# A feed-forward block with one product fewer by recursion: a product moved back, a fixed order on the matrix engine, and four row tiles prepared later

## The chip, the core and the metric

The kernel runs on one core of a Trainium2 chip. The core has a matrix engine (TensorE, "PE" in the profile, with its weight loads as "PEld"), a vector engine (VectorE, "DVE"), a scalar engine (ScalarE, "ACT"), a general engine (GpSimd, "POOL") and a queue that issues transfers (SyncE, "SP"). Each has its own list of instructions and works through it in order; semaphores tie the lists together. PE writes to a small memory of its own with banks (PSUM), which DVE and ACT read. The metric is the time of one execution on the device in microseconds (us); lower is better.

## What is computed

One layer of a transformer-like block over 2048 rows of 1024 numbers. Two kinds of attention come first; their heads' outputs are joined, multiplied by an output matrix and added to the input. Then comes the part that this document is about:

```
u2   = rms_norm(h, norm2_w)             # 2048 x 1024
gate = u2 @ w_gate                       # 1024 x 2816
up   = u2 @ w_up                         # 1024 x 2816
h    = h + (silu(gate) * up) @ w_down    # 2816 x 1024
```

The answer is asked for in 32-bit floating point. The kernel gets near that on 16-bit matrix products by splitting every operand into a high and a low half (hi + lo) and adding three products: hi*hi, hi*lo and lo*hi.

## The kernel before, in words

The attention part and the output projection fill the time up to about 1427 us. What follows is the feed-forward. The 2816 hidden columns are taken in 11 groups of 256, and the 2048 rows in two halves of 1024, so there are 22 steps: groups 0 to 10 for the first half, then the same for the second (the list `steps`, the loop variable `i`).

**Seven products for eight.** In each step, gate and up are each a product of 1024 x 1024 by 1024 x 256, cut into 2 x 2 blocks. A scheme after Strassen and Winograd forms it with seven block products, at the price of sums of the blocks before and after. `quad` issues the seven for gate or for up: `pa`, `p6`, `p7`, `pd`, then one more added into the bank of `pa`, `p4`, and a seventh added into the bank of `pd`. Each block product is twelve matmuls (four slices of the depth, three pairs of halves), all issued by `product`. Between them DVE adds and subtracts: L1047 after the second product, L1052 after the third, L1057 after the fourth (it reads `pd`, and the seventh product may only add into that bank after this), L1067 after the sixth, L1071 after the seventh. Silu of the gate is on ACT (L1083), the product of gate and up on DVE (L1103), and the result is split into an `act` tile (two buffers) by ACT casts and subtractions on POOL or DVE (L98).

**Down.** Each time two groups have their `act` (after the gate of the next step), `down` multiplies both by their `w_down` blocks, again with seven block products, for four row groups j of 256 rows; a block product is three matmuls for each group ("unit"), so six here. The down at the change of the halves has one unit, the last has three. Its products are named `pa`, `pb`, `pc`, `pd`, one more into `pa`, one more into `pd`, and `pe`. DVE adds the banks onto tiles `hs` with rows of h (L1144), which SP loads from memory and stores back (L1128, L1187); there are four such tiles, two for each j.

**Weights.** In the first half, every group's three weight blocks are fetched, scaled, summed and split (`load_ffn`: squares on ACT L954 or L190 into the one `sq` tile, column sums `fsc` on PE L963, splits on ACT L216 and DVE L221, sums on POOL L98), a group ahead of their use, and stored; in the second half they are fetched back ready. Gate and up weights share two buffers (tag wgu), down weights have two (tag wd). The steps of this work hang on hooks: `quad` calls `at(1)` to `at(7)` after its products, and `in_gate` and `in_up` then advance the chains of the next weights.

**Late rows.** The normalized, transposed and block-summed rows (X) come from memory; for the last four row tiles (12 to 15) they are made during the feed-forward by the generator `build_x`, in two passes of two tiles. Each `tick` advances it by one `yield`: load, norm, transposes on PE (L1213), then casts, subtractions and stores to the memory tensor `xcd`. It uses the four `hs` tiles and, as a 16-bit buffer, one of the two wd buffers. `late_at` names the hooks of the first two steps at which it ticks. X of the second half is loaded at the twelfth step (`load_x`, L1225) into the same tiles as that of the first half, in the order `XL = (0, 4, 5, 1, 2, 6, 3)`; each tile is free when the last product of the first half that reads it is done.

**Order.** The program is written in a framework that turns it into the lists of the engines by simulating it: an instruction goes out when the simulation has it ready, the one written first ahead of others. So the products need not run in the order in which they are written. `tc.issue_after(x)` adds an edge: instructions within it come later than x on the same engine, without a wait. Before, only the column sums and transposes stand in such edges (`behind()`, which refers to `front[0]`, the last matmul issued), and the products themselves are free.

Of the kernel before, what the change touches and what calls it, by code (L numbers as in the profile page):

```python
# [40 lines left out]
CU = 3  # L41
# [18 lines left out]
def block(tc, a, out):  # L60
# [3 lines left out]
    with top:  # L64
# [809 lines left out]
        with ExitStack() as ph2:  # L874
# [21 lines left out]
            rows = []  # L896
# [8 lines left out]
            def stage(fg, nme):  # L905
                st = stages[:, turn[0]]
                turn[0] ^= 1
                f0 = 256 * fg
                with tc.issue_after(rows[1].ins) if (fg, nme) == (1, "u") else nullcontext():
                    fetch(st, f0, nme)  # L910
                store(0)
                return st
# [113 lines left out]
            def product(ps_, wv, wo, X, xo, start, stop):  # L1026
                q = 0
                for kt in range(4):
                    for xi, wi in ((0, 0), (1, 0), (0, 1)):
                        front[0] = PE.matmul(ps_[:].rearrange("p (t n) -> p t n", n=P), lhsT=wv[:, wo, wi, 128 * kt : 128 * kt + 128], rhs=X[xo][:, :, xi, kt, :], start=start and q == 0, stop=stop and q == 11, skip_group_check=not start).ins  # L1030
                        q += 1

            def quad(wv, X, tag, bufs, c11, hooks):
# [13 lines left out]
                DVE.tensor_tensor(u2[:], p6[:], u2[:], ALU.add)  # L1047
                at(2)
# [21 lines left out]
                product(pd, wv, 5, X, 3, False, True)  # L1070
                DVE.tensor_tensor(u2[:], u2[:], pd[:], ALU.add)  # L1071
                c11(0, 1, u2)
                at(7)

            def gate(W, X, hooks):
# [10 lines left out]
                quad(W["g"], X, "cg", 5, on_gate, hooks)  # L1086
                note("A", 2000)
                return sg

            def up(W, X, sg, hooks, final=False):  # L1090
                if final:
                    act = stages[:].rearrange("p b n -> p (b n)").bitcast(F16)[:, :7168].rearrange("p (o s n) -> p o s n", o=7, s=2)
                else:
                    act = fp.tile([P, 7, 2, 512], F16, tag="act", bufs=2, name=nm("act"))
# [23 lines left out]
                quad(W["u"], X, "cu", CU, on_up, hooks)  # L1118
# [12 lines left out]
            def down(half, units, hs, last, hook=None):  # L1131
# [3 lines left out]
                def prod(po, ao, wo, j, start=True):  # L1135
                    for u, (W, act) in enumerate(units):
                        for q, (xi, wi) in enumerate(((0, 0), (0, 1), (1, 0))):
                            front[0] = PE.matmul(po[:], lhsT=act[:, ao, xi, 128 * j : 128 * j + 128], rhs=W["d"][:, wo, wi, :], start=start and u == 0 and q == 0, stop=u == nu - 1 and q == 2, skip_group_check=not start).ins  # L1138
# [13 lines left out]
                for j in range(4):  # L1152
# [14 lines left out]
                    acc(u2[:], pb, u2[:])  # L1167
                    pc = pst("pd")
# [177 lines left out]
```

## Time and profile before

| | us |
|---|---|
| median of three runs | 2686.87 |
| lowest, highest | 2677.16, 2687.23 |
| the profiled execution | 2682.59 |
| its span, first to last instruction | 2680.8 |
| PE busy in the span | 2492.4 (93%) |
| DVE busy | 1932.7 (72%) |
| POOL busy | 1489.1 (56%) |
| ACT busy | 1347.0 (50%) |
| granted PE clock, mean | 0.984 |

The profile is that of one execution. A matmul's row starts when it is issued, and matmuls overlap, so that the start of the next row tells more than the length of one. Idle time before an instruction is put down to what ended it. The chain of work that ended last lies on PE for 39% of the span in the rows that the page sums up, most of it in the products of lines 1030 (gate and up) and 1138 (down).

### The profile page before, as it was taken

The page shows a single profiled execution, that of the slowest core. Times are in us where ns is not written, and L with a number is a line of the kernel's source. Part 1 is how long each engine was busy: PE and PEld are TensorE (multiplying, and loading weights), DVE is VectorE, ACT ScalarE, POOL GpSimd, SP SyncE. Part 2 cuts the span into 40 slices and gives each one's busy share as a digit, 9 for nine tenths or more (in the row PEclk, how much of TensorE's full clock was granted, in tenths as well). Part 3 has the DMA queues.
Part 4 walks back from the last instruction along what each step waited for, and adds up shares of the span by engine and source line. Part 5 has one row for each costly group of instructions (what it writes and reads, how often), then busy time and mean ns, then how long its engine had stood idle before and what let it go on. Part 6 is the DMA issues. An engine that isn't in the chain of part 4 may idle for free. (4 is left out here: it accounts for less than half of the span.)

```text
span 2680.8 us, 50579 instructions
## 1 busy us (share of the span) xinstructions
PE 2492.4 (93%) x19628; PEld 1498.6 (56%) x19628; DVE 1932.7 (72%) x3711; ACT 1347.0 (50%) x2487; POOL 1489.1 (56%) x1098
## 2 busy tenths in 40 slices
PE   6998989888988989889989899999999999999999
PEld 4655656577776776557775344444444444444444
DVE  6898969898989989877766868777685544444434
ACT  4665656567978878665644535344352112111121
POOL 2578667667767766546764656565564232322323
PEclk9999999999999999999999899999999999999999
DMA  6777697767998979987897574665649743635532
GB/s 222 213 162 181 146 200 168 179 143 184 193 179 179 185 160 209 210 191 217 218 285 282 208 250 178 255 226 202 245 183 346 293 177 143 233 141 186 195 111 95
DMA packets 619585, 534.41 MB, mean 199 GB/s; under 512 B 480640, under 2 KB 548224, under 8 KB 609104
## 3 DMA queue, kind: packets, MB, share of 16 engines
q1 hardware_dynamic: 617520, 529.09, 69.9%
q8 instruction: 154, 2.52, 0.4%
q0 software_dynamic: 512, 1.36, 0.2%
q14 instruction: 87, 0.71, 0.1%
q10 hardware_dynamic: 1312, 0.72, 0.1%
HBM read 261.08 MB, written 147.32 MB: 152 GB/s over the span
## 5 line engine op out<-in xcount | busy, mean ns | idle before, releaser
L98 POOL TENSOR_TENSOR s<-z,s 128x1024 f16<-128x1024 f32 (+7 forms) x288 | 472.0, 1647 | 142.5 <-ACT s L89 109.8
L507 PE MATMUL sc<-kT,qT 128*128 128x512 f16 (+3 forms) x1520 | 382.0, 353 | 53.3 <-DVE z L623 19.3
L622 DVE TENSOR_TENSOR_SCAN z<-z,sc 128x512 f32<-128x512 f32 (+3 forms) x320 | 352.8, 1112 | 58.6 <-ACT sc L620 38.0
L1138 PE MATMUL pd<-wd,act 128*128 128x512 f16 x1764 | 390.9, 379 | 1.2 <-DVE cg L1071 1.2
L326 PE MATMUL pj<-w,xt 128*128 128x384 f16 x1920 | 352.2, 331 | 18.8 <-ACT xt L683 6.9
L1030 PEld LDWEIGHTS <-wg 128*128 128x128 f16 x1848 | 182.0, 99 | 230.2 <-issue 16.4
L518 PE MATMUL yp<-v,aT 128*128 128x64 f16 (+1 forms) x4896 | 269.8, 204 | 41.6 <-DMA aT<-s 40.2
L518 PEld LDWEIGHTS <-aT 128*128 128x128 f16 x4896 | 237.5, 99 | 120.4 <-DMA aT<-s 52.5
L1030 PEld LDWEIGHTS <-wu 128*128 128x128 f16 x1848 | 180.7, 98 | 218.0 <-issue 2.6
L98 POOL TENSOR_TENSOR act<-cg,act 128x512 f16<-128x512 f32 x112 | 148.5, 1337 | 262.9 <-ACT act L1097 150.8
L1138 PEld LDWEIGHTS <-act 128*128 128x128 f16 x1764 | 172.8, 98 | 209.4 <-issue 2.8
L326 PEld LDWEIGHTS <-xt 128*128 128x128 f16 x1920 | 187.3, 99 | 147.5 <-issue 21.4
L89 ACT CAST s<-z 128x128 f16<-128x128 f32 (+7 forms) x215 | 173.1, 809 | 134.1 <-DMA aT<-s 40.5
L98 POOL TENSOR_TENSOR hs<-hs,cu 128x512 f32<-128x512 f32 x99 | 130.9, 1328 | 171.3 <-DVE hs L1144 70.8
L619 ACT ACTIVATE z<-sc,c 128x512 f32<-128x512 f32 (+3 forms) x320 | 210.7, 663 | 25.6 <-PE sc L507 11.7
L1097 ACT CAST act<-cg 128x512 f16<-128x512 f32 x126 | 77.3, 616 | 238.4 <-DVE cg L1103 162.7
L507 PEld LDWEIGHTS <-qT 128*128 128x128 f16 x1520 | 128.4, 99 | 121.0 <-DVE z L623 23.0
L832 PE MATMUL po<-wo,mt 128*128 128x256 f16 x1536 | 180.7, 277 | 13.9 <-DVE xf L835 8.4
L1030 PE MATMUL pm<-X,wu 128*128 128x512 f16 x792 | 180.4, 379 | 1.3 <-DVE wu L221 1.3
L1030 PE MATMUL pm<-X,wg 128*128 128x512 f16 x792 | 181.3, 382 | 0.0
L342 PE MATMUL pj<-xt,w 128*128 128x128 f16 x2304 | 175.0, 220 | 6.7 <-DVE v L364 5.7
L1144 DVE SCALAR_TENSOR_TENSOR hs<-pd,c,hs 128x512 f32<-128x512 f32 x136 | 99.0, 747 | 109.6 <-PE pd L1138 83.1
(266 smaller groups left out, 4737.6 us busy)
## 6 DMA issues: line engine op xcount, KB each, us to landing
xt<-xs SPq DMA_DIRECT2D x112, 512.0 KB, 4.3
hs<-hd SPq DMA_DIRECT2D x68, 512.0 KB, 4.5
hd<-hs SPq DMA_DIRECT2D x56, 512.0 KB, 4.7
split<-wg SPq DMA_DIRECT2D x11, 1792.0 KB, 7.8
split<-wu SPq DMA_DIRECT2D x11, 1792.0 KB, 6.7
split<-wd SPq DMA_DIRECT2D x11, 1792.0 KB, 7.2
wg<-split SPq DMA_DIRECT2D x11, 1792.0 KB, 7.3
wd<-split SPq DMA_DIRECT2D x11, 1792.0 KB, 12.2
```

Of the source, the lines that this page charges most:

```text
L89: ACT.copy(dst, src)
L98: (DVE if e == "D" else POOL).tensor_tensor(dst, a_, b_, op)
L326: PE.matmul(pj[:, :384], lhsT=xv[:, xi, kt, :], rhs=G["w"][:, wi, kt, :], start=n == 0, stop=n == 23)
L342: PE.matmul(o, lhsT=x_ if c == 2 else w_, rhs=w_ if c == 2 else x_, start=n == 0, stop=n == 23)
L507: last = PE.matmul(sc[:, : 128 * w].rearrange("p (t n) -> p t n", n=P), lhsT=G["q"][i // 4][:, a_, i % 4, :], rhs=G["k"][q][:, b_, 0:w, :] ...
L518: PE.matmul(yp[:, y0 : y0 + wd], lhsT=aT[:, a_, :], rhs=v[:, v_ : v_ + wd], start=start and j == 0 and q == 0, stop=stop and j == nb - 1 a ...
L619: ACT.activation(om[:, lo:hi], sc[:, :w], AF.Sigmoid, scale=G["nkz"][:])
L622: DVE.tensor_tensor_scan(ov, ov, sc[:, :w], om[:, hi : hi + 1], op0=ALU.mult, op1=ALU.bypass)
L832: PE.matmul(po[:, sl], lhsT=mt[:, kt, P * xi : P * xi + P], rhs=wos[2 * h + n][wi][:, kt, :], start=q == 0, stop=q == 23)
L1030: front[0] = PE.matmul(ps_[:].rearrange("p (t n) -> p t n", n=P), lhsT=wv[:, wo, wi, 128 * kt : 128 * kt + 128], rhs=X[xo][:, :, xi, kt, : ...
L1138: front[0] = PE.matmul(po[:], lhsT=act[:, ao, xi, 128 * j : 128 * j + 128], rhs=W["d"][:, wo, wi, :], start=start and u == 0 and q == 0, s ...
L1144: DVE.scalar_tensor_tensor(dst, po[:], kd[:], src, op0=ALU.mult, op1=ALU.add)
```

## The change

Three edits go together.

1. `quad` hands the seventh product back as a function (`seventh`) when called with `late=True`, which `gate` does. It is run behind the second product of what follows: of `down` at j = 0 where a down is due, else of `up`. The hook `at(7)` of the gate comes before it.
2. `product` and down's `prod` issue all their matmuls within `behind()`. So every block product is issued on PE after the one written before it.
3. `build_x` ticks in steps 2 to 5 (the third to sixth group) and not in 0 and 1. Each pass takes its four `hs` tiles anew, fetches the gain anew, and uses the `act` tile of the step as its 16-bit buffer, which `up` then takes over (`acts`), in place of a wd buffer. The first tick before the loop is gone, and so is the edge that held the fetch of the second group's up weights behind the late rows' loads.

```diff
             def product(ps_, wv, wo, X, xo, start, stop):
                 q = 0
-                for kt in range(4):
-                    for xi, wi in ((0, 0), (1, 0), (0, 1)):
-                        front[0] = PE.matmul(ps_[:]..., lhsT=wv[...], rhs=X[xo][...], ...).ins
-                        q += 1
+                with behind():
+                    for kt in range(4):
+                        for xi, wi in ((0, 0), (1, 0), (0, 1)):
+                            last = PE.matmul(ps_[:]..., lhsT=wv[...], rhs=X[xo][...], ...)
+                            q += 1
+                front[0] = last.ins
...
                 DVE.tensor_tensor(u2[:], p6[:], u2[:], ALU.add)
+                if before is not None:
+                    before()
                 at(2)
...
-                product(pd, wv, 5, X, 3, False, True)
-                DVE.tensor_tensor(u2[:], u2[:], pd[:], ALU.add)
-                c11(0, 1, u2)
+                def seventh():
+                    product(pd, wv, 5, X, 3, False, True)
+                    DVE.tensor_tensor(u2[:], u2[:], pd[:], ALU.add)
+                    c11(0, 1, u2)
+                if not late:
+                    seventh()
                 at(7)
+                return seventh
...
                     acc(u2[:], pb, u2[:])
+                    if before is not None and j == 0:
+                        before()
...
             def build_x():
-                w2f, xa, xb, xt = (hp.tile([P, D], F32, tag="hs", bufs=4, name=nm("bx")) for _ in range(4))
-                b16 = fd.tile([P, 7, 2, 512], F16, tag="wd", bufs=2, ...)
...
                 for j in (2, 3):
+                    w2f, xa, xb, xt = (hp.tile([P, D], F32, tag="hs", bufs=4, name=nm("bx")) for _ in range(4))
                     for q, z in enumerate((xa, xb)):
-                        rows.append(SP.dma_start(z[:], hd[8 + 2 * j + q]))
+                        SP.dma_start(z[:], hd[8 + 2 * j + q])
+                    SP.dma_start(w2f[:], a["norm2_w"].partition_broadcast(P))
                     yield
...
+                    acts.append(new_act())
                     yield from x_ops([d2(z) for z in (xa, xb)], d2(xt), 1, j, bufs, "AP", "DP")
+                    yield
...
-            tick(1)
             load_now(0, 0, "d", W)
...
-            late_at = ((5, 9, 10, 11, 12, 13, 14), (3, 7, 8, 9, 10, 11, 12))
+            late_at = {2: (9, 11, 13), 3: (1, 2, 3, 4, 5), 4: (9, 11, 13), 5: (1, 2, 3, 4, 5)}
...
-                sg = gate(W, X, in_gate)
+                sg, seventh = gate(W, X, in_gate)
...
                 if due:
-                    down(dh, units, hs, dh != half, lambda: go("g"))
-                    units = []
-                act = up(W, X, sg, in_up, not more)
+                    down(dh, units, hs, dh != half, lambda: go("g"), seventh)
+                    units, seventh = [], None
+                act = up(W, X, sg, in_up, not more, seventh)
```

In `late_at`, numbers up to 7 are the gate's hooks and from 8 on those of up (7 is added).

More of the change, by code (lines that the diff above doesn't have):

```diff
@@ L894, in block @@
             scales = {}
-            rows = []
             front = [None]
@@ L908, in stage @@
                 f0 = 256 * fg
-                with tc.issue_after(rows[1].ins) if (fg, nme) == (1, "u") else nullcontext():
-                    fetch(st, f0, nme)
+                fetch(st, f0, nme)
                 store(0)
@@ L1093, in up @@
                 else:
-                    act = fp.tile([P, 7, 2, 512], F16, tag="act", bufs=2, name=nm("act"))
+                    act = acts.pop() if acts else new_act()
                 def put(o, src):
@@ L1129, in load_hs, with down @@
                 return h
-            def down(half, units, hs, last, hook=None):
+            def down(half, units, hs, last, hook=None, before=None):
                 kd = units[-1][0]["kd"]
```

31 lines of the change are left out of this document (17 added, 14 removed).

## The prediction

> **What bounds the kernel now.** I read the page first, then a table of busy time by stage, then PE's own timeline, and last the groups of instructions by line.
>
> ```profile
> PE 2492.4 (93%) x19628; PEld 1498.6 (56%) x19628; DVE 1932.7 (72%) x3711; ACT 1347.0 (50%) x2487; POOL 1489.1 (56%) x1098
> ...
> 1427.00:1521.00 94.00, 85.46 (x415) 41.21 (x414) 72.66 (x98) 51.15 (x66) 54.18 (x36) 0.96 0.60 216
> ...
> 1746.00:2060.00 314.00, 309.82 (x1467) 144.38 (x1466) 228.60 (x348) 135.24 (x160) 177.30 (x128) 0.99 0.63 232
> 2060.00:2676.00 616.00, 616.00 (x2855) 279.16 (x2853) 271.34 (x356) 108.46 (x172) 187.28 (x148) 1.00 0.49 182
> sum 1249.00, PE 1228.55 PEld 566.23 DVE 739.42 ACT 396.88 POOL 548.28; mean PE 204.76 PEld 94.37 DVE 123.24 ACT 66.15 POOL 91.38
> ```
>
> The columns of the table are the stretch, its length, then PE, PEld, DVE, ACT and POOL busy, the granted clock, the DMA share and GB/s. The feed-forward runs from 1427 to 2676. PE is its bound: 1228.55 of 1249.00 us busy, and from 2060 on, which is the second half of the rows, not idle at all. So the second half can only lose, and the first holds 1249.00 - 1228.55 = 20.45 us of idle PE. Where that lies, PE's timeline tells (start, length, what, and in brackets the idle time before it with what ended it):
>
> ```profile
> 1466.50 2.75 PE L1030 MATMUL pd<-X,wu 128*128 128x512 f16 x12 [1.36 <-DVE cu L1057]
> ...
> 1491.13 4.76 PE L1030 MATMUL pd<-X,wg 128*128 128x512 f16 x12 [5.47 <-DVE cg L1057]
> ...
> 1533.90 1.87 PE L963 MATMUL fsc<-sq,ones 128*128 128x256 bf16 x8 [5.88 <-ACT sq L954]
> 1535.56 7.34 PE L1030 MATMUL pm<-X,wg 128*128 128x512 f16 x24
> ...
> 1549.37 1.03 PE L963 MATMUL fsc<-sq,ones 128*128 128x256 bf16 x8
> ...
> 1773.91 4.13 PE L1030 MATMUL pd<-X,wg 128*128 128x512 f16 x12 [3.30 <-DVE cg L1057]
> 1777.84 3.10 PE L1138 MATMUL pd<-wd,act 128*128 128x512 f16 x12
> ...
> L1030 PE MATMUL pd<-X,wg 128*128 128x512 f16 x528 | 124.9, 387 | 9.9 <-DVE cg L1057 8.9 <-DMA X<-xcd 1.0
> L1030 PE MATMUL pd<-X,wu 128*128 128x512 f16 x528 | 121.5, 379 | 2.0 <-DVE cu L1057 2.0
> L1138 PE MATMUL pd<-wd,act 128*128 128x512 f16 x1764 | 390.9, 379 | 1.2 <-DVE cg L1071 1.2
> L1030 PE MATMUL pm<-X,wu 128*128 128x512 f16 x792 | 180.4, 379 | 1.3 <-DVE wu L221 1.3
> 2621.80 54.41 PE pd L1138 x252
> ```
>
> The last row is from the chain: 54.41 / 252 = 0.216 us a matmul, so a product of twelve takes 2.59 us and one of six 1.30. A product of twelve without a wait shows 2.75 in the timeline (the 1466.50 row, after only 1.36 us of idle). After the long waits it shows 4.76 and 4.13: the array is slow for a while, and that is paid on top: 2.01 after 5.47; 1.38 and 0.35 after 3.30; 0.84 (1.87 against 1.03) and some 2.0 after 5.88 (24 matmuls in 7.34, where two products take 5.2 plus 0.16). Sum of the slowness 6.6, so 20.45 + 6.6 = 27 us is all that there is to win.
>
> **The change, part by part: what it can win.** The seventh gate product adds into the bank of the fourth (pd), which DVE must first read (L1057). Behind it now stand two products more: 5.2 us of slack beside an up product, 2.6 us beside a down product. The gate's pd group waits 9.9 us in all, the two largest being 5.47 and 3.30, and the second has only down's two short products in front: 2.6 us against 3.30, so 0.7 might stay. With the slowness, 9.9 + 2.01 + 1.73 = 13.6; I take 13. The 1.2 of the down group goes too, as the bank of the seventh is no longer the one waited for.
>
> The wait of 5.88 is the column sums of the third group's up weights. Their squares (L954) use the one sq tile, which the second group's down weights hold, and these were late because the late rows' 16-bit buffer held a wd slot. The buffer is now an act tile and the late rows come later, so this goes: 5.88 + 2.84 = 8.7. The waits of up's pd product (1.36 and a smaller one, 2.0 in all) are in the two groups that lose the late rows; I take half, 1. The 1.3 at wu L221 I take as gone, since in order the up products come later than where it stood. Win: 13 + 1.2 + 8.7 + 1 + 1.3 = 25.2.
>
> **What the edges cost at the half boundary.** Before, the order on PE was free, and where X of the second half was late, products of down stood between those of the gate:
>
> ```profile
> 2067.37 2.75 PE L1030 MATMUL pd<-X,wg 128*128 128x512 f16 x12
> 2069.96 4.05 PE L1138 MATMUL pd<-wd,act 128*128 128x512 f16 x18
> 2073.86 2.75 PE L1030 MATMUL pa<-X,wg 128*128 128x512 f16 x12
> 2076.45 2.75 PE L1138 MATMUL pd<-wd,act 128*128 128x512 f16 x12
> 2079.04 2.75 PE L1030 MATMUL pm<-X,wg 128*128 128x512 f16 x12
> 2081.63 6.64 PE L1138 MATMUL pd<-wd,act 128*128 128x512 f16 x30
> 2088.10 2.75 PE L1030 MATMUL pd<-X,wg 128*128 128x512 f16 x12
> ...
> 2056.37 1.16 SPq L1225 DMA_DIRECT2D X<-xcd  x2
> ...
> 2064.55 0.32 SPq L1225 DMA_DIRECT2D X<-xcd  x1
> ...
> X<-xcd SPq DMA_DIRECT2D x1, 1024.0 KB, 17.5
> ...
> X<-xcd SPq DMA_DIRECT2D x1, 1024.0 KB, 21.1
> ```
>
> The last two rows are the answers for the issues at 2056.37 and 2064.55 alone: they land after 17.5 and 21.1 us, at 2073.9 and 2085.65. In order, the gate's fifth product would start at 2069.96 and waits for X until 2073.9: 3.9 us. The sixth then ends at 2079.05. Down's two products of this group have one unit, three matmuls each (1.3 us together), so the seventh is due at 2080.35 and waits until 2085.65: 5.3 us. Waits of 3.30 and 5.47 brought 1.7 and 2.0 us of slow matmuls above, so 9.2 + 3.7 = 12.9. Bounds: 0, if the transfers are issued in another order, and 15, if other transfers come first. I take 12: the transfers and what frees their buffers are not changed.
>
> **What the edges cost in down.** Within a row group j, pd's second product must wait until DVE has added its first (acc on hs), with one product of 1.30 us between, and all that is behind it on PE waits too. When DVE or the hs tile is late, the old order put something else there:
>
> ```profile
> 1659.49 9.66 PE L1138 MATMUL pd<-wd,act 128*128 128x512 f16 x44
> ...
> 1697.92 1.46 PE L1138 MATMUL pd<-wd,act 128*128 128x512 f16 x6
> ...
> 1678.92 1.84 DVE L221 SCALAR_TENSOR_TENSOR wg<-sq,c,wg 128x1024 f16<-128x1024 f32 x1
> ...
> 1694.38 1.41 DVE L1144 SCALAR_TENSOR_TENSOR hs<-pd,c,hs 128x512 f32<-128x512 f32 x2 [3.21 <-DMA hs<-hd]
> ...
> L1144 DVE SCALAR_TENSOR_TENSOR hs<-pd,c,hs 128x512 f32<-128x512 f32 x136 | 99.0, 747 | 109.6 <-PE pd L1138 83.1 <-DMA hs<-hd 26.3
> ```
>
> DVE's adds waited 26.3 us for hs transfers, and PE none of it. In the down that starts at 1659.49, the add of the third row group would be due after the seventh gate product, 14 products of j = 0 and 1 and four of j = 2: 2.59 + 18 x 1.30 = 26.0, with column sums of 0.9 (1.03 less 0.16) between, at 1686.4. It ran at 1694.38, 8 us later, and a product of down was put off to 1697.92 behind up's. But hs waits for the store of j = 0, and that was late for the very reason that j = 0's product had been put off. In order it is stored sooner by most of the 8 us. So a down with two units in the first half (there are five) loses between 0 and 8 us, 0 to 40 in all. DVE's weight splits (1.84 above) between two adds can hold one up by some 1 us more. I take 1.5 a down, 7.5: nearer to 0, because the cause of the lateness goes with the order. In the second half DVE is busy 271 of 616 us, and I take 0; the slack of one product over the add is 1.30 - 0.75 = 0.5 us there, and if DVE were late by more, each of 20 row groups would pay the rest.
>
> **What the late rows cost where they go.** Moved are, twice, three transfers (the norm's gain is now fetched twice), two squares, two powers on POOL, two scalings, 16 transposes on PE with four copies on ACT, the casts and subtractions, and four stores on SP.
>
> ```profile
> L229 DVE SCALAR_TENSOR_TENSOR bx<-bx,xrs,bx 128x1024 f32<-128x1024 f32 x4 | 8.5, 2127 | 0.5 <-POOL xrs L156 0.3
> L98 DVE TENSOR_TENSOR b<-bx,b 128x1024 f16<-128x1024 f32 (+1 forms) x5 | 9.4, 1891 | 1.5 <-ACT b L89 1.5
> L221 DVE SCALAR_TENSOR_TENSOR wu<-stages,c,wu 128x1024 f16<-128x1024 f32 x22 | 38.3, 1766 | 4.4 <-ACT wu L216 4.4
> L221 DVE SCALAR_TENSOR_TENSOR wd<-stages,c,wd 128x1024 f16<-128x1024 f32 x22 | 27.7, 1279 | 1.4 <-ACT wd L216 1.0
> ...
> hs<-hd SPq DMA_DIRECT2D x68, 512.0 KB, 4.5
> ```
>
> PE's share (32 transposes) is moved, not added. DVE's subtractions into the 16-bit buffer (9.4 us for both) now stand in the gates of the fourth and sixth group, in front of the split of the up weights, and up's second product needs that split 2.6 us sooner, as the seventh gate product now stands behind it. That is where PE waited for wu before (1.3). Bounds: 0, and 9.4 + 8.5 = 18 if all of DVE's moved work came before the split. I take 2 for each of the two groups, 4, and 1 for transposes that wait for late hs tiles. On SP the late rows' loads wait for down's last stores to free the hs tiles, and the weight fetches and split stores queued behind them wait too. A load takes 4.5 us to land; weights are fetched a group ahead, so I take nothing, and without that lead it would be 4.5 us twice. The gain's second fetch is covered by a DMA share of 0.6.
>
> The same split form takes 1.77 us for wu and 1.28 for wd. The Trainium skill (GPSIMD Engine Reference, Specifications) says that GpSimd shares its SBUF interfaces with VectorE and contends with instructions that have two SBUF inputs. The rows agree that some of these run slow, and do not tell why. By the page more POOL work beside the splits would stretch them by up to 0.5 us each, four splits in two groups, an estimate of 4 us more, and the sum would end at 2687.
>
> **The end.**
>
> ```profile
> 2676.23 0.75 DVE L1144 SCALAR_TENSOR_TENSOR hs<-pd,c,hs 128x512 f32<-128x512 f32 x1 [0.47 <-PE pd L1138]
> ...
> L98 DVE TENSOR_TENSOR hs<-hs,cu 128x512 f32<-128x512 f32 x3 | 2.1, 691 | 0.1
> ```
>
> The last add on DVE belonged to a product that had been put off; in order the last product is another one, whose add has one more of 0.69 us behind it: +0.7.
>
> **Sum.** 2682.59 (the profiled run's own time) - 25.2 + 12 + 7.5 + 5 + 0.7 = 2682.6. The median of the three runs shown, 2686.87, is 4.3 above the profiled one, and the lowest 2677.16 is below it, so 0.5% (13 us) is about what a measurement of this kernel can tell from no change.
>
> **The rivals.** *Faster:* the free order, not the data, made down's waits, and X comes in time or nearly so, as the transfers are issued sooner. Then only 5 or so of the 25 us of costs stay: 2682.6 - 25.2 + 5 = 2662. For it: the waits that the trace shows are few, and the two causes behind 22 of the 27 us are taken away; against it: the landings at 2073.9 and 2085.65 hang on nothing that the change moves. *Slower:* in order, each of the five downs waits for its hs tiles. At 6 us a down, 30 in place of 7.5: 2705. It decides from 4.2 us a down on, where the sum passes 2696. For it: 26.3 us of hs waits on DVE; against: those waits are partly the order's own work. *The change does not do what it says, the seventh's wait only changes its place:* the same late DVE holds up the next product that needs it, the weights of up (L221); then the 13 us stay and the sum gives 2695.6.
>
> **How the numbers follow.** The forecast, gains and costs that nearly cancel, gets 0.35, its own range being 2670 to 2696; the faster rival 0.31; the slower 0.29; the changed place 0.05, which lies within 0.5% too, by a hair. So faster 0.31, same 0.40, slower 0.29. The range reaches from near the whole gain, 2661, to the slower rival with some of the upper bounds, 2712.
>
> **What would show it.** Right: the gate's pd group without idle time; no column sums with 5.88; PE idle at the first gate after the half boundary, ended by X, 9 us in two waits; idle on down's products in the first half, ended by DVE hs. Wrong: waits in down of 5 us or more each, a wait of the transposes for hs, or PE idle in the second half behind 2100, where I expect none.

## The result, and the profile after

The changed kernel takes 2762.45 us, the median of five executions (2758.12 to 2772.13), against 2681.49 (2677.16 to 2687.23, five executions) of the kernel before. The ratio is 1.031, with a 95% interval from 1.028 to 1.033: slower by 81 us, and outside the predicted range. The profiled execution took 2758.12 us, its span is 2756.3, and its mean granted PE clock 0.976 (0.984 before).

The first line is the page's busy time by engine. The rows behind it are the table by stage over the feed-forward (stretch, length, PE, PEld, DVE, ACT and POOL busy, granted clock, DMA share, GB/s), which now lies between 1423 and 2752.

```profile
PE 2511.8 (91%) x19628; PEld 1502.9 (55%) x19628; DVE 1934.2 (70%) x3711; ACT 1346.9 (49%) x2488; POOL 1484.4 (54%) x1098
...
1423.00:1746.00 323.00, 293.09 (x1376) 136.96 (x1374) 221.32 (x328) 139.97 (x170) 165.75 (x119) 0.96 0.56 207
1746.00:2100.00 354.00, 314.37 (x1452) 145.11 (x1452) 236.67 (x359) 143.37 (x169) 187.89 (x133) 0.95 0.56 201
2100.00:2150.00 50.00, 40.59 (x169) 17.27 (x168) 20.30 (x31) 11.83 (x17) 11.00 (x8) 0.90 0.91 364
2150.00:2752.00 602.00, 598.76 (x2770) 270.86 (x2768) 262.70 (x343) 102.14 (x162) 179.86 (x142) 1.00 0.48 168
sum 1329.00, PE 1246.80 PEld 570.20 DVE 740.99 ACT 397.31 POOL 544.50; mean PE 311.70 PEld 142.55 DVE 185.25 ACT 99.33 POOL 136.12
```

The feed-forward grew from 1249 to 1329 us. Idle time of PE went from 20.45 to 1329.00 - 1246.80 = 82.2 us, and its busy time from 1228.55 to 1246.80: the same matmuls, 18.3 us slower in all. The number of instructions on DVE (3711) and POOL (1098) is unchanged, and all of the loss lies in the first half and at the boundary; from 2150 on PE is idle for 3.2 us in 602. The groups of PE's instructions in that stretch say what it waits for (busy, mean ns | idle time before, and what ended it):

```profile
L1152 PE MATMUL pd<-wd,act 128*128 128x512 f16 x1764 | 394.7, 382 | 18.5 <-DVE hs L1159 16.9 <-DVE stages L1159 1.6
...
L1029 PE MATMUL pa<-X,wu 128*128 128x512 f16 x528 | 125.6, 389 | 9.4 <-ACT wu L216 9.1 <-DVE wu L221 0.3
...
L1029 PE MATMUL pd<-X,wg 128*128 128x512 f16 x528 | 122.8, 383 | 2.5 <-DMA X<-xcd 2.5
L1029 PE MATMUL pd<-X,wu 128*128 128x512 f16 x528 | 121.5, 379 | 0.0
L961 PE MATMUL fsc<-sq,ones 128*128 128x256 bf16 x160 | 24.0, 300 | 44.0 <-ACT sq L952 44.0
```

The waits that the change aimed at are gone: the gate's `pd` group no longer waits for DVE (8.9 us before), nor does up's `pd` (2.0). In their place stand 44.0 us before the column sums `fsc` (5.88 before), 18.5 before down products (1.2), 9.4 for X at the boundary (1.0; three waits, shown further below), and 9.4 before up's first product (none). The column sums' wait is spread over 13 of the 20 sums of gate's and up's weights, with 13.03 us as the longest; before, it was a single one.

How a down product comes to wait is best read from the chain of waits, around the second largest case (start, length, what):

```profile
1679.25 9.40 DMA hd<-hs
...
1688.67 5.03 DMA hs<-hd
...
1693.79 0.76 DVE hs L1159
...
1694.60 5.57 PE pd L1152 x13
```

A finished row tile is stored (9.40 us), then the next rows are loaded into the same tile (5.03), then DVE may add, and only then may PE go on. Before the last of these rows PE's timeline has an idle time of 5.05 us.

### The profile page after: what moved, and what is told of

It reads as the page before. It is cut to its first block, busy times and chain, and to the rows that moved or that the text cites. A ratio compares the mean times of both kernels' runs of the same rounds, so it can differ in the third digit from the quotient of the medians.

```text
span 2756.3 us, 50648 instructions
## 1 busy us (share of the span) xinstructions
PE 2511.8 (91%) x19628; PEld 1502.9 (55%) x19628; DVE 1934.2 (70%) x3711; ACT 1346.9 (49%) x2488; POOL 1484.4 (54%) x1098
## 4 chain that ended last, share of the span: by engine, by line
PE 36%; DVE 7%; DMA 4%; ACT 2%; issue 1%; POOL 1%; SPq 0%; DVEq 0%; ACTq 0%; POOLq 0%
PE pd L1152 11%; PE pm L1029 10%; PE pd L1029 7%; PE pa L1029 6%; DVE wu L221 2%; DMA hd<-hs 2%; PE po L832 1%; DMA X<-xcd 1%; DVE wd L221 1%; ACT sq L952 1%; PE fsc L961 1%; DMA hs<-hd 1%; DVE act L98 1%; DVE cg L1116 1%; DVE cg L98 0%
## 5 line engine op out<-in xcount | busy, mean ns | idle before, releaser
L1152 PE MATMUL pd<-wd,act 128*128 128x512 f16 x1764 | 394.7, 382 | 18.5 <-DVE hs L1159 16.9
L98 POOL TENSOR_TENSOR act<-cg,act 128x512 f16<-128x512 f32 x114 | 156.3, 1383 | 245.5 <-issue 154.4
L543 DVE TENSOR_SCALAR_CACHE_REDUCE z<-sc,c 128x512 f32<-128x512 f32 (+3 forms) x256 | 160.8, 646 | 15.5 <-PE sc L507 14.4
```

Source lines behind the costliest of these rows:

```text
L98: (DVE if e == "D" else POOL).tensor_tensor(dst, a_, b_, op)
L543: DVE.tensor_scalar(z[:, lo : lo + f], sc[:, :f], kz_d[:], None, op0=ALU.mult, op1=ALU.max, accum_out=mx[:, m, nx : nx + 1])
L1152: last = PE.matmul(po[:], lhsT=act[:, ao, xi, 128 * j : 128 * j + 128], rhs=W["d"][:, wo, wi, :], start=start and u == 0 and q == 0, stop= ...
```

## The experiments

Ratios are to the kernel before, executed beside them on the same chip, with 95% intervals. "Idle" is PE's idle time in the feed-forward's groups. The edges on gate's and up's products stand in `product`, those on the downs in down's `prod`. The diffs show only the lines that make the point; where a part of the change is left out, its other lines too are as in the kernel before.

### One part of the change at a time

**Only the seventh product moved**: the new `quad`, `gate`, `up` and the calls of `seventh`, without edges, late rows as before.

```diff
             def product(ps_, wv, wo, X, xo, start, stop):
-                with behind():
+                if True:
...
                 def prod(po, ao, wo, j, start=True):
-                    with behind():
+                    if True:
```

> Only the seventh gate product is moved; the products' order is free and the late rows stay in the first two groups. Theory 1 (the late rows in the gates of the fourth and sixth group are the cause): the 9.9 us of the gate's pd group go, nothing comes, -5 to -15 us against before. Theory 2 (the edges are the cause): the same, -5 to -15. Theory 3 (the moved seventh frees the gate's weights later, so the next weights are late and PE waits at their column sums): column sums wait by 20 us or more, +10 to +40.

Measured: 2678.07 us against 2678.68, ratio 0.9997 (0.9987 to 1.0006). In a free order the moved product is worth nothing, which none of the three expectations had; the gate's `pd` group still waits for DVE, 5.5 us.

**Only the edges**, on all products; the seventh in its old place, late rows as before.

```diff
             def quad(wv, X, tag, bufs, c11, hooks, before=None, late=False):
+                late = False
...
                 at(7)
-                return seventh
+                return None
```

> Only the edges: all products in the order in which they are written, seventh product and late rows as before. Theory 1: the half boundary (some 12 us) and down's waits for hs (16 us in the changed kernel), +15 to +30 us, and column sums wait no longer than before (7 us). Theory 2: column sums wait by 25 us or more in all, spread over the groups, and the total is +35 to +60. Theory 3: +15 to +30.

Measured: 2738.25 us, ratio 1.0228 (1.021 to 1.0245): +60 us. Downs wait 19.5 us, column sums 17.7, the gate's `pd` 12.3 for DVE and 4.7 for X. The time is that of the second theory; the sums' wait is not, which it had at 25 us or more.

**Only the late rows** taken in the third to sixth group, with the changed `build_x`.

```diff
-            late_at = ((5, 9, 10, 11, 12, 13, 14), (3, 7, 8, 9, 10, 11, 12))
+            late_at = {2: (9, 11, 13), 3: (1, 2, 3, 4, 5), 4: (9, 11, 13), 5: (1, 2, 3, 4, 5)}
```

> Only the late rows: taken in the third to sixth group, the order of the products free, the seventh gate product as before. Theory 1: PE waits by 15 us or more in the fourth and sixth group for column sums or up weights, +15 to +40 us. Theory 2: the free order puts other products there, -10 to +5. Theory 3: -10 to +5.

Measured: 2693.57 us, ratio 1.0056 (1.004 to 1.0073): +15 us. The column sums' wait falls to 2.9, but the gate's `pd` group waits 15.4, of which 5.28 and 6.88 us stand in the fourth and sixth group, where DVE's part of the late rows went. The first theory had these groups and nearly the time, but not which product waits.

**Seventh and edges**, late rows as before.

```diff
-            late_at = {2: (9, 11, 13), 3: (1, 2, 3, 4, 5), 4: (9, 11, 13), 5: (1, 2, 3, 4, 5)}
+            late_at = {0: (5, 9, 10, 11, 12, 13, 14), 1: (3, 7, 8, 9, 10, 11, 12)}
```

> The seventh moved and the edges, the late rows as before in the first two groups. Theory 1: half boundary and down's waits alone, +10 to +25 us. Theory 2: near the whole, +45 to +75, with column sums waiting 30 us or more. Theory 3: +45 to +75, and more than the edges alone by 20 or more.

Measured: 2753.61 us, ratio 1.0281 (1.0266 to 1.0297): +75 us. The gate's `pd` no longer waits for DVE at all, yet 15 us more are lost than with the edges alone: the column sums wait 37.5 us in place of 17.7. The moved product does what it is meant to, and more than it saves comes back in front of the sums. The edges are the main cause; which of them, the next pair tells.

### Which edges

In both runs the seventh product and the late rows are as before.

**Edges on gate and up alone.**

```diff
                 def prod(po, ao, wo, j, start=True):
-                    with behind():
+                    if True:
```

> The kernel before with the fixed order for the gate's and up's products alone; the down products stay free. Theory 'parts add': of the 60 us of the edges, about 20 are the downs' waits for the rows that VectorE prepares; they go and 35 to 45 us stay, ratio 1.013 to 1.017, idle before column sums and the gate's fourth product as with all edges (18 and 17 us). Rival 'downs set it': the downs' delays push the gate and up out of step with their loads; without edges on the downs nearly all of it goes, ratio below 1.007.

**Edges on the downs alone.**

```diff
             def product(ps_, wv, wo, X, xo, start, stop):
-                with behind():
+                if True:
```

> The kernel before with the fixed order for the down products alone; gate and up stay free. Theory 'parts add': 15 to 25 us, ratio 1.006 to 1.009, all of it idle time before down products that VectorE ends. Rival 'downs set it': 45 us or more, ratio 1.017 or above, with waits before column sums and the gate's products too. Third way, that a free gate and up fill the downs' waits: ratio within 1.003.

Measured: on gate and up 2682.96 us against 2683.51, ratio 0.9999 (0.9984 to 1.0014); on the downs 2741.22 us, ratio 1.0203 (1.0172 to 1.0234), +58 us. The first expectation of each fell: it is the downs, and with them alone come waits before the column sums and the gate's products as well. The third of the second run fell too: the free products of gate and up did not fill the downs' waits. The order is settled when the program is built, by the simulation, and on the chip PE keeps to it: it stands idle for 5.87 us at 1702.47, before down products, with up's first product 36 matmuls further on in its list. PE's groups with edges on gate and up alone, then with edges on the downs alone:

```profile
L1156 PE MATMUL pd<-wd,act 128*128 128x512 f16 x1764 | 390.1, 379 | 0.0
...
L963 PE MATMUL fsc<-sq,ones 128*128 128x256 bf16 x160 | 21.5, 279 | 10.9 <-ACT sq L954 10.9
```

```profile
L1156 PE MATMUL pd<-wd,act 128*128 128x512 f16 x1764 | 401.7, 386 | 15.4 <-DVE hs L1163 14.6 <-DVE stages L1163 0.5 <-ACT cu L1183 0.2
L1031 PE MATMUL pm<-X,wg 128*128 128x512 f16 x792 | 180.4, 381 | 1.6 <-DMA X<-xcd 1.6
L1031 PE MATMUL pd<-X,wg 128*128 128x512 f16 x528 | 129.4, 397 | 17.9 <-DVE cg L1063 12.1 <-DMA X<-xcd 5.8
L1031 PE MATMUL pa<-X,wg 128*128 128x512 f16 x528 | 123.3, 382 | 3.9 <-DMA X<-xcd 3.9
L963 PE MATMUL fsc<-sq,ones 128*128 128x256 bf16 x160 | 23.2, 294 | 20.6 <-ACT sq L954 20.6
```

So down's products were the filler of the whole first half: free, they are put wherever something else is late; fixed, they wait themselves, and little fills the other waits. The down group is also 11.6 us slower in its busy time.

### What the fixed downs wait for

**Without the stores** of the first half's rows by the downs (what its groups before the last add to these rows is lost), edges on the downs alone; and the same without any edges.

```diff
-                    for q in range(2):
+                    for q in range(2 if half or last else 0):
                         t = 8 * half + 2 * j + q
                         SP.dma_start(out[...] if last else hd[t], hs[j][q][:])
```

> Edges on the downs alone, and the first half's downs do not store their rows of the residual sum to DRAM (the sums of the first half's groups before the last are lost), so that the four row buffers come free as soon as VectorE and GpSimd are done with them. Theory 'ring of rows': in the fixed order a down's matmuls wait for VectorE, which waits for the next rows, whose load waits until the store of the rows before has landed; without the store 10 us or more of the 15 us before down products go, and with the slow matmuls behind them the time falls by 12 to 25 us: ratio 1.011 to 1.016. Rival 'VectorE's queue': VectorE is simply late with the evictions of the product before, the waits stay within 3 us of 15, ratio 1.018 to 1.023.

> The kernel before (free order) without the first half's stores of the residual rows by the downs; their sums are lost. Theory 'ring of rows': in the free order TensorE runs other products while the rows come back, so the ring costs it at most the 1 us of idle time before down products: ratio 0.997 to 1.000. Rival 'traffic': the stores slow the other transfers too, and leaving them out helps any order: ratio 0.990 to 0.995.

Measured: 2716.03 us, ratio 1.0128 (1.0093 to 1.0163), 23 us less than with the stores. In the free order the stores cost nothing: ratio 0.9999 (0.9984 to 1.0015). Without them the fixed downs wait 4.5 us in place of 15.4, and the waits for X fall from 11.3 to 4.1:

```profile
L1156 PE MATMUL pd<-wd,act 128*128 128x512 f16 x1764 | 396.7, 382 | 4.5 <-DVE hs L1163 3.9 <-DVE stages L1163 0.5
L1031 PE MATMUL pd<-X,wg 128*128 128x512 f16 x528 | 128.2, 394 | 16.2 <-DVE cg L1063 12.1 <-DMA X<-xcd 4.1
...
L963 PE MATMUL fsc<-sq,ones 128*128 128x256 bf16 x160 | 23.1, 293 | 19.3 <-ACT sq L954 19.3
```

The ring of four row tiles is thus shown as one cause of the downs' waits. The 23 us are not all the ring's: 7.2 us of idle time went at the waits for X. Leaving out the stores takes transfers away as well, and the run doesn't part the two. Nor is the ring the column sums' cause: these wait 19.3 us still.

**The boundary of the halves**: edges on the downs, but not on that down.

```diff
+                last_half = half == 0 and nu == 1
...
-                    with behind():
+                    with nullcontext() if last_half else behind():
```

> Edges on the downs alone, but not on the single group's downs at the half boundary, where the free order lets TensorE run them between the first products of the second half while its operands are still being loaded. Theory 'boundary counts': the three waits for X there (10 us with the edges on all downs) and the slow matmuls behind them go, 12 to 20 us less than with edges on all downs: ratio 1.013 to 1.016. Rival 'X late anyway': the loads of X only start when the first half's last readers are done, so the waits stay and the ratio stays at 1.018 to 1.023.

Measured: 2727.97 us, ratio 1.0176 (1.0139 to 1.0212). The trace shows the waits for X fall from 11.3 to 2.6 us, but the time's interval overlaps that with all the downs fixed (from 1.0172), so that the 11 us between the two losses are not settled as a size; the ratio lies between the two expectations.

**The column sums behind two down products**, edges on the downs alone; `lag[0]` is 1 in a group with downs, else 0.

```diff
                         ACT.activation(sq[:], st, AF.Square)
+                        if nme == "g":
+                            for _ in range(lag[0]):
+                                yield
...
                     acc(u2[:], pb, u2[:])
+                    if hook is not None and j == 0:
+                        hook()
```

> Edges on the downs alone, and in a group with downs the next gate weights' column sums are emitted behind down's second product, not ahead of its first. Theory 'sums ahead of the downs': with the downs fixed behind them, the sums stop all of the downs when the square is 3 to 5 us late; behind a few down products they are covered: idle before column sums falls from 20.6 to 8 to 12 us, ratio from 1.020 to 1.013 to 1.016. Rival 'late chain': the sums wait as long where they are now, or the next sums do; ratio 1.017 to 1.023.

**All three taken away together.**

> Edges on the downs alone with three things taken away at once: the first half's stores of the residual rows (their sums are lost), the edge on the downs at the half boundary, and the column sums ahead of the downs. If these three are the causes of the 58 us: ratio 1.000 to 1.006. If something else in the fixed downs costs about as much as before: ratio 1.008 to 1.013.

Measured: with the sums later 2730.34 us, ratio 1.0191 (1.0173 to 1.0209); the sums wait 15.8 us in place of 20.6, so two products more are far from enough, as the rival had it. With all three 2699.91 us, ratio 1.008 (1.0059 to 1.0101): 39 of the 58 us are accounted for, and 19 are left, so that the three are not the whole cause. Of the waits left, 15.9 us stand before column sums (5.88 before the change) and 12.1 before the gate's `pd` for DVE (8.9). What these lack, PE's timeline shows at the second down, first in the kernel before, then in this one:

```profile
1656.90 2.75 PE L1030 MATMUL pd<-X,wg 128*128 128x512 f16 x12
1659.49 9.66 PE L1138 MATMUL pd<-wd,act 128*128 128x512 f16 x44
1668.99 1.04 PE L963 MATMUL fsc<-sq,ones 128*128 128x256 bf16 x8
```

```profile
1652.26 2.75 PE L1035 MATMUL pd<-X,wg 128*128 128x512 f16 x12
1654.85 2.75 PE L1161 MATMUL pd<-wd,act 128*128 128x512 f16 x12
1662.04 1.87 PE L967 MATMUL fsc<-sq,ones 128*128 128x256 bf16 x8 [4.43 <-ACT sq L955]
```

The squares are ready 9.8 us after the gate's last product starts (1652.26 to 1662.04). In the kernel before 44 matmuls of down lay in between and PE noticed nothing; here it is twelve, and PE waits 4.43 us. Such waits are 10 of the 19 us by the sums' groups, and 3 more are the gate's `pd`; what the rest is stays open.

### Why the moved seventh costs once the order is fixed

**The changed kernel with free downs.**

```diff
                 def prod(po, ao, wo, j, start=True):
-                    with behind():
+                    if True:
```

> The changed kernel with the edge taken from the down products alone; gate's and up's edges, the moved seventh product and the late rows stay. Theory 'downs': the fixed order of the downs is the main cause, as it was with the edges alone (58 us with it, none with gate and up alone), so 55 to 70 us go and the late rows' 10 to 20 us stay: ratio 1.003 to 1.010. Rival 'sum of small things': with the seventh and the late rows added, the gate's and up's edges cost by themselves what they did not cost alone: ratio above 1.015.

**The same with the late rows as before**: seventh moved, edges on gate and up.

> The kernel before with the seventh product moved and the edges on gate and up alone; rows where they were, downs free, column sums at their old step. If the gate's wait for its own second sum (11 to 12 us before its fourth product) is really removed by the moved seventh, and nothing takes its place: ratio 0.994 to 0.997. If the wait only changes its place to the column sums, as with edges everywhere: ratio 0.999 to 1.004, with 15 us or more before the column sums.

Measured: 2721.89 us, ratio 1.0142 (1.0113 to 1.0172), and 2705.24 us, ratio 1.0087 (1.0053 to 1.012). Both lie outside the ranges of their two expectations; the second has the sign that its rival named, 15 us or more before the sums. The moved seventh and the edges on gate and up cost nothing alone (0.9997 and 0.9999), and together they cost 24 us. Most of the new waiting is before the column sums, 28.6 us in place of 10.9 with the edges on gate and up alone; the late rows' transposes wait 7.0 in place of 1.3. How the sums come to wait, PE's and ACT's timelines show at one of them, with the edges on gate and up alone, and then with the seventh moved as well:

```profile
1727.35 2.75 PE L1031 MATMUL pm<-X,wg 128*128 128x512 f16 x12
1731.79 2.75 PE L1031 MATMUL pd<-X,wg 128*128 128x512 f16 x12 [1.68 <-DVE cg L1063]
1735.56 1.03 PE L963 MATMUL fsc<-sq,ones 128*128 128x256 bf16 x8 [1.02 <-ACT sq L954]
...
1733.60 1.91 ACT L954 ACTIVATE sq<-stages 128x2048 bf16<-128x2048 f32 x1 [0.47 <-DVE wu L221]
```

```profile
1728.42 2.75 PE L1031 MATMUL pm<-X,wg 128*128 128x512 f16 x12
1736.64 1.86 PE L963 MATMUL fsc<-sq,ones 128*128 128x256 bf16 x8 [5.46 <-ACT sq L954]
...
1734.68 1.91 ACT L954 ACTIVATE sq<-stages 128x2048 bf16<-128x2048 f32 x1 [0.47 <-DVE wu L221]
```

The square starts 6.3 us after the gate's sixth product in both. With the seventh in its place, PE spends the time on 1.68 us of waiting for DVE, on the product, and on 1.02 of waiting for the square. Without it, PE reaches the sums sooner and waits 5.46, and its matmuls are slow behind that. The product that was moved away because it waited was the cover of a longer chain: the splits of up's weights (DVE, L221) must be done before the one `sq` tile takes the next square.

**The column sums of gate's and up's weights two calls later**, first in the changed kernel, then with the seventh moved and edges on gate and up.

```diff
                         ACT.activation(sq[:], st, AF.Square)
                         note("A", 1900)
+                        yield
+                        yield
                     yield
```

> The changed kernel, all three parts kept, with the step of the weight loading that emits the column sums (and the splits behind it) two calls later, so that a gate's or up's column sums stand about two products further back in TensorE's list. Theory 'place': the 44 us of idle time before the column sums come from where they stand in the fixed list, ahead of a square that the rest of the kernel cannot deliver sooner; then these waits fall below 10 us, nothing of that size takes their place, and the time falls by 30 to 45 us, to a ratio of 1.014 to 1.019. Theory 'late chain': the whole loading of the next weights (square, sum, splits) runs too late, and whatever reads it waits; then the waits before the column sums go too, but 25 to 40 us come back before the first products with the new weights (wg, wu, ended by ScalarE's or VectorE's splits), and the ratio stays at 1.026 to 1.034.

> The kernel before with the gate's seventh product moved, the fixed order for gate's and up's products alone, and the column sums two calls later; downs free, late rows where they were. Theory 'place': the wait of the gate's fourth product (12 us in the kernel before) is gone by the moved seventh, the column sums no longer wait, the downs fill their own waits: ratio 0.994 to 1.001. Theory 'late chain': the waits come back before the products with new weights: ratio 1.010 to 1.020.

**The next gate weights' sums alone, one product later**, with the seventh moved and edges on gate and up; then two later in groups without downs; then one later in the changed kernel. `lag` is as above, 1 (or 2) in groups without downs too, and in down the hook is called behind `before()`.

> The second candidate (seventh moved, edges on gate and up, downs free) with the next gate weights' column sums alone emitted one step later: behind up's first product, and in a group with downs behind the moved seventh. Theory 'cover': the moved seventh took away the one product that stood between the gate's sixth and the sums; with another product in its place the 28.6 us before the column sums fall to 8 to 16, and the ratio from 1.009 to 0.998 to 1.004. Rival 'late chain': the splits behind the sums start later by as much, the waits come back before up's or gate's first product, ratio 1.006 to 1.012.

> As the run with one step, but two more products (behind the moved seventh) in the groups without downs too. Theory 'cover': column sums wait under 8 us, ratio 0.995 to 1.002. Rival 'late chain': the up's weights, whose square waits for the gate's splits, come late: waits before the down weights' scale, the up's sums or up's first product of 10 us or more, ratio 1.005 to 1.012.

> The changed kernel with the next gate weights' column sums one product later, as in the first of these runs. Theory 'cover': of the 44 us before the column sums 15 to 25 go, ratio from 1.031 to 1.020 to 1.026; the downs' waits (18 us) and the boundary's (9 us) stay. Rival 'late chain': nothing gained, ratio 1.027 to 1.034.

Measured: all sums later, 2763.81 us, ratio 1.030 (1.028 to 1.032), no gain, and 2710.06, ratio 1.0096 (1.0077 to 1.0115). The gate's sums alone: one later 2696.32, ratio 1.0051 (1.0033 to 1.0068); two later 2703.4, ratio 1.008 (1.0055 to 1.0104); in the changed kernel 2756.22, ratio 1.0277 (1.0253 to 1.03). PE's groups of the changed kernel with all sums later show why putting them off isn't free:

```profile
L1031 PE MATMUL pm<-X,wu 128*128 128x512 f16 x792 | 191.4, 394 | 6.7 <-DVE wu L221 4.5 <-ACT wu L216 2.1
...
L1031 PE MATMUL pa<-X,wu 128*128 128x512 f16 x528 | 123.9, 384 | 10.7 <-ACT wu L216 5.6 <-DVE wu L221 5.0
...
L963 PE MATMUL fsc<-sq,ones 128*128 128x256 bf16 x160 | 23.0, 292 | 16.3 <-ACT sq L952 16.3
...
L183 PE MATMUL fsc<-id,m 128*128 128x128 f32 x22 | 5.3, 326 | 21.2 <-ACT sq L190 21.2
```

The sums wait 16.3 us in place of 44.0, but the scale of the down weights (L183, no wait before) waits 21.2, and up's products 17.4 for their splits. Neither theory holds alone. Sums that stand later wait less, but little of that reaches the time. One product later, the waits before them go from 28.6 us to 21.5 and the loss from 24 us to 13, each against the kernel before beside it; the two intervals overlap (1.0053 to 1.012, 1.0033 to 1.0068), so that the 11 us are no settled size. In the changed kernel the waits go from 44.0 to 27.0 and the loss from 81 to 73, with overlapping intervals too, while up's first product waits 15.3 in place of 9.4. The rest comes back in the loading chain itself, square, sum, splits, next square, which passes through one `sq` tile: with the gate's sums two later, they wait only 5.2 us, but the scale of the down weights waits 12.5.

No version tried is faster than the kernel before; the best two, at 0.9997 and 0.9999, cannot be told from it.

## Why the prediction was wrong, point by point

Built up from the kernel before, the medians go: edges on gate and up +0, with the seventh moved +24, with the late rows +41, with the downs fixed +81. In idle time of PE and against the prediction's terms:

| term | predicted | measured idle |
|---|---|---|
| gate's `pd`, as it waited before (8.9 for DVE, 1.0 for X) | -9.9 | -9.9 |
| up's `pd`; wu L221 | -1; -1.3 | -2.0; -1.3 |
| column sums | -5.9 | +38.1 |
| X at the boundary | +9.2 | +9.4 |
| downs (+7.5, and the 1.2 of before gone) | +6.3 | +17.3 |
| late rows at up's products | +4 | +9.4 |
| late rows' transposes | +1 | 0 |
| second half | 0 | 0 behind the boundary |

The measured column adds up to 61 of the 61.8 us. The matmuls took 18.3 us longer in all, where the prediction had their slowness behind waits fall by 6.6 and rise by 3.7. At the end the last product's add on DVE has one more of 0.69 us behind it, as forecast.

*The column sums* are the step that failed: "this goes: 5.88 + 2.84 = 8.7". The cause given for the third group's wait was plausible, since with the late rows alone the sums wait 2.9 us. But the question what covers the sums in all the other groups wasn't asked. Before, these stood behind the gate's seventh or behind up to 44 down matmuls; the change moves the one away and fixes the others, and 13 of the 20 sums wait for their square in place of one. The prediction put that cost at nothing, without a reason. The trace of before held the numbers: the square's end and the sums' start could have been set against the new list of products.

*The seventh's wait* did go, as said, for the gate, once the edges held the seventh where it was written. The rival "the seventh's wait only changes its place" was right in kind and got 0.05; it named up's weights as the next to wait, and it was the sums. It had the 13 us merely stay, so no gain; with edges on gate and up the moved seventh costs 24 us, since the chain that the sums wait for was longer than the wait removed (5.46 us in place of 1.68 and 1.02 above).

*The boundary*: right. Three waits for X, not two, of 9.41 us, and slow matmuls of 5.30 - 2.75 + 2.90 - 2.75 + 4.45 - 2.75 = 4.4: 13.8 in all, against 12.

```profile
2124.91 2.76 PE L1029 MATMUL pm<-X,wg 128*128 128x512 f16 x12 [2.29 <-DMA X<-xcd]
...
2134.83 5.30 PE L1029 MATMUL pa<-X,wg 128*128 128x512 f16 x12 [4.57 <-DMA X<-xcd]
2139.93 2.90 PE L1029 MATMUL pm<-X,wg 128*128 128x512 f16 x12
...
2146.67 4.45 PE L1029 MATMUL pd<-X,wg 128*128 128x512 f16 x12 [2.55 <-DMA X<-xcd]
```

*The downs*: 17.3 us of idle time lie within the bounds of 0 to 40, but the value was taken near the wrong end, because of the step "In order it is stored sooner by most of the 8 us". Here are SP's issues at the second down, before and after:

```profile
1680.79 0.32 SPq L919 DMA_DIRECT2D split<-wg  x1
1681.45 2.88 SPq L1187 DMA_DIRECT2D hd<-hs  x3
1690.47 2.77 SPq L1128 DMA_DIRECT2D hs<-hd  x3
```

```profile
1678.12 0.32 SPq L917 DMA_DIRECT2D split<-wg  x1
1679.25 7.80 SPq L1204 DMA_DIRECT2D hd<-hs  x3
1688.67 2.85 SPq L1141 DMA_DIRECT2D hs<-hd  x3
```

The first of these stores goes out 2.2 us sooner and the loads 1.8, not 8, and the down's first product itself started 1.3 us sooner: the row store is issued right behind the store of the split gate weights (1792 KB) and takes 9.40 us to land. The slower rival, "each of the five downs waits for its hs tiles", had the mechanism; it lacked that a fixed down also uncovers the sums, so that the downs' edges cost 40 us on top of the rest. Two of the five downs wait over 5 us (5.05 and 5.46), a sign that the prediction had named for being wrong.

*The late rows* cost 6 us on top of the seventh and all edges, 17 without the downs' edges and 15 alone, against 5 and bounds of 0 to 18: mis-sized. The cause named, DVE's moved work in front of the split of the up weights, fits the places, but not 2 us a group. In the fourth group up's first product waits 9.13 us. In the sixth the same delay reaches the next square and its sum: 13.03 us, where the run with the seventh moved, all edges and the late rows as before has 5.47 (last line). By these two rows, some 7 of the column sums' 38 us are the late rows', an estimate.

```profile
1615.02 1.03 PE L1029 MATMUL pa<-X,wu 128*128 128x512 f16 x2 [9.13 <-ACT wu L216]
...
1758.56 1.86 PE L961 MATMUL fsc<-sq,ones 128*128 128x256 bf16 x8 [13.03 <-ACT sq L952]
```

```profile
1749.72 1.87 PE L963 MATMUL fsc<-sq,ones 128*128 128x256 bf16 x8 [5.47 <-ACT sq L954]
```

The estimate from the GPSIMD Engine Reference (the Trainium skill, Specifications), that the splits of up's weights would be stretched by more POOL work beside them, did not come true: in the feed-forward their mean went from 1815 ns before to 1738 after. But the rule itself was hardly tried. In the fourth and sixth group the four splits of this form took 1277 to 1284 ns, and POOL was idle beside nearly all of that (1615.2 to 1618.2, 1751.7 to 1757.9).

```profile
L221 DVE SCALAR_TENSOR_TENSOR wu<-stages,c,wu 128x1024 f16<-128x1024 f32 x20 | 35.8, 1815 | 4.4 <-ACT wu L216 4.4
```

```profile
L221 DVE SCALAR_TENSOR_TENSOR wu<-stages,c,wu 128x1024 f16<-128x1024 f32 x20 | 34.1, 1738 | 4.7 <-ACT wu L216 4.6
```

## What to carry to other kernels

Before a product is moved because it waits, look up what stands behind it in the engine's list and how late that would be without it: a product that waits 2 us can cover a chain that is 6 us late. Fixing the order of the work that fills gaps (here the downs) costs in all the places that it filled, not only in its own waits, so leave the filler free (the edges on gate and up alone cost nothing here). And when a step is put off to give its input time, follow the chain behind it by one period first.

## What was not expected of the hardware

A wait of less than 3 us can make the matmuls behind it slow, or not, and the slowness can come late. From the run with the sums one later, and from the one without:

```profile
1975.76 1.86 PE L967 MATMUL fsc<-sq,ones 128*128 128x256 bf16 x8 [2.89 <-ACT sq L955]
```

```profile
1769.01 1.03 PE L963 MATMUL fsc<-sq,ones 128*128 128x256 bf16 x8 [3.71 <-ACT sq L954]
1769.88 4.44 PE L1031 MATMUL pm<-X,wg 128*128 128x512 f16 x12
```

Eight column sums take 1.86 us in place of 1.03 after 2.89 us of waiting; after 3.71 us they take 1.03, and it is the product behind them that takes 4.44 in place of 2.75. In the run with edges alone, 2.41 us are enough for 1.87 (at 1921.90). At the boundary 2.29 us slowed nothing. The Trainium skill (TensorE: Matmul & The Clock Gate, Part 1) has the clock fall after an idle window of about 3.4 us that runs freely; a free-running window agrees with the scatter, but the cases of 2.89 and 2.41 us are shorter than the idle window it names, and here the measurement decides. In the feed-forward after, PE's busy time is longer than before by 18.3 of the 80 us; that all of it is such slowness is not shown.
